# A Strassen-type MLP in a one-core decoder layer: paddings, weight sums in place, another order of products

## The chip, the cores and the metric

The kernel runs on one core of a Trainium2 chip. The metric is the device time of one execution in microseconds (us). A second figure is the span, from the first to the last instruction that the profiler recorded; one profiled execution gives both.

## The reference

One decoder layer in float32 with 1024 tokens and 1024 channels: x += gate1 * Mixer(h), x += gate2 * MLP(h), and a last RMSNorm. The part that the change is about:

```python
h = rmsnorm(x, norm2_g[l]) * (1.0 + scale2) + shift2
x = x + gate2 * (jnp.square(jax.nn.relu(h @ mlp_w1[l])) @ mlp_w2[l])     # 1024 -> 4096 -> 1024
return rmsnorm(x, final_g)
```

The mixer runs four branches (gated DeltaNet, pooling, spatial gating, retention) on one input projection, multiplies each branch's output by a sigmoid gate of the same input, adds them up and projects the sum.

## The kernel before

Everything lies channel by token: a tile is 128 channels of 512 tokens ("half" hf is 0 or 1). Each float32 operand is split into a rounded high part (ScalarE copy into float32r) and a low rest (VectorE subtraction), and a product is three matmuls: high by high, high by low, low by high (`mm3` at L125, L415 in the mixer, `product` at L1125).

Order of the stages: input projection, pooling and spatial gating; the mixers, whose short chains on VectorE and TensorE are filled up with matmuls of the projection (L415); `branches`, 64 units of a gate (24 matmuls, hh or hl by whi or wlo) and a branch product (12 matmuls, yh or yl by bh or bl); `outproj`; `mlp`.

The MLP uses Winograd's form of Strassen's scheme: in a 2 x 2 block product seven products take the place of eight. The operand sets b11, t3, n2, b21, n1, t4, b22 are sums of blocks of the activations (high and low parts, four tiles of 128 x 512 each), and a11, s3, s2, a12, s1, a22, s4 are sums of blocks of the weights. One product is 12 matmuls into a PSUM bank. `up` runs 16 units (p), each making a pair of 128-row blocks of the hidden layer for both halves; it squares the positive part, forms the sums that the second layer needs and stores them in DRAM (`ad`). `down` runs 4 x 4 units (c: quarter of the hidden layer, m: pair of output blocks); at each c the seven operand sets are loaded and split again (`load`, `put`). For p below NE (5) the products a11 x b11 and a12 x b21 run before the units, while VectorE still builds the other operand sets, and their results wait in `early` and in DRAM.

Weights come in `wpair` as two loads of 512 KB; s3 and s1 are added on VectorE, s2 and s4 on GpSimd (L1102), and each operand is split when its product is issued, into one of seven pairs of buffers (wh, wl). In `down`, `snap` scales a bank on ScalarE into v and adds v to x1 on GpSimd (L1137); x1 itself was saved to DRAM by `outproj` and is loaded again before `down`.

A scheduler orders each engine's instructions at build time, by program order among those that its model holds ready; on the chip each queue (SP's, which issues nearly all DMAs, among them) runs in that fixed order and waits on semaphores.

Pools are stacked from both ends of a partition. Their first bytes, as the program allocates them:

| pool | holds | first byte | beyond a multiple of 128 |
|---|---|---|---|
| cp (left) | small constants, rowb | 16,512 | 0 |
| bp | hh, hl, mh, ml, operand sets (tag h) | 21,120 | 0 |
| s4, later mp, later xb | plh, pll; mixer tiles; yh, yl, x1, operand sets (tag b16) | 86,656 | 0 |
| pb (right) | bh, bl, sig and others of `branches`, `outproj` | 159,616 | 0 |
| pm (right) | raw, wh, wl, st, early | 153,536 | 64 |
| wp (right) | raw, whi, wlo | 204,736 | 64 |

Of the kernel before, what the change touches and what calls it, by code (L numbers as in the profile page):

```python
# [63 lines left out]
def layout(x, c, positions, norm1_g, norm2_g, ada_w, ada_b, w_in, dn_conv_w, dn_a_log,  # L64
# [18 lines left out]
    o["w1"] = tiles(A["mlp_w1"][0])  # L83
    o["w2"] = ct(A["mlp_w2"][0].reshape(4, 4, 2, P, NB, P).transpose(0, 4, 3, 2, 1, 5).reshape(4, NB, P, 1024))
# [13 lines left out]
class Trunk:  # L98
# [90 lines left out]
    def start(self):  # L189
# [4 lines left out]
        self.rowb = cp.tile([P, 520], FP32, name="rowb")  # L194
# [822 lines left out]
    def outproj(self):  # L1017
# [7 lines left out]
        for hf in range(2):  # L1025
# [15 lines left out]
            ps = self.pss()  # L1041
            nc.tensor.matmul(out=ps, lhsT=self.one, rhs=ssq, start=True, stop=True)
            if hf == 0:
                rs = bp.tile([P, 512], FP32, tag="rs", name="rs", bufs=2)
                self.rms(ps, rs)
                self.S = {"b11": self.opset(self.xb, "b16"), "b21": self.opset(self.xb, "b16")}
        self.ps_rs = ps
# [4 lines left out]
    def put(self, op, k, x):  # L1052
        hi, lo = self.S[op][:, 0, k], self.S[op][:, 1, k]
        self.nc.scalar.copy(out=hi, in_=x)  # L1054
        self.nc.vector.tensor_tensor(out=lo, in0=x, in1=hi.bitcast(FP32), op=ALU.subtract)  # L1055
# [12 lines left out]
    def h2_rest(self, k, rs):  # L1068
        nc = self.nc
        self.h2_raw(1, k, rs, nc.vector)  # L1070
        self.h2_raw(1, k + 4, rs, nc.gpsimd)
        x11, x21, x12, x22 = self.x1[0][:, k], self.x1[0][:, k + 4], self.x1[1][:, k], self.x1[1][:, k + 4]
        tt = lambda eng, o, a, b: eng.tensor_tensor(out=o, in0=a, in1=b, op=ALU.subtract)
# [3 lines left out]
        tt(nc.vector, x11, x11, x12)  # L1077
        neg(n2, x22, x11)
        self.put("n2", k, n2)
        tt(nc.gpsimd, x12, x22, x12)  # L1080
        self.put("t3", k, x12)
        self.put("n1", k, x11)
        neg(x21, n2, x21)
        self.put("t4", k, x21)


    def st(self, name):
        return self.pm.tile([P, 512], FP32, tag="st", name=name, bufs=7)

    def wpair(self, s0, s1):  # L1090

        nc, pm = self.nc, self.pm
        r = []
        for s in (s0, s1):
            r.append(pm.tile([P, 1024], FP32, tag="raw", name="raw", bufs=2))
            nc.sync.dma_start(out=r[-1], in_=s)
        a11, a12, a21, a22 = r[0][:, :512], r[0][:, 512:], r[1][:, :512], r[1][:, 512:]
        src = {"a11": a11, "a12": a12, "a22": a22}

        def sums():  # L1100
            s = {n: pm.tile([P, 512], FP32, tag="sg", name=n, bufs=4) for n in ("s3", "s1", "s2", "s4")}
            add = lambda eng, o, a, b: eng.tensor_tensor(out=o, in0=a, in1=b, op=ALU.add)  # L1102
            add(nc.vector, s["s3"], a11, a21)
            add(nc.vector, s["s1"], a21, a22)
            add(nc.gpsimd, s["s2"], s["s1"], a11)
            add(nc.gpsimd, s["s4"], s["s2"], a12)
            src.update(s)

        def get(n):
            if n[0] == "s" and n not in src:  # L1110
                sums()
            hi = pm.tile([P, 512], FR, tag="wh", name="wh", bufs=7)
            lo = pm.tile([P, 512], FR, tag="wl", name="wl", bufs=7)
            self.split(src[n], hi, lo)
            return hi, lo
        return get
# [17 lines left out]
    def mlp(self):  # L1134
        nc, A, pm = self.nc, self.A, self.pm
        NP, NE = 16, 5
# [3 lines left out]
        OPS = ("b11", "t3", "n2", "b21", "n1", "t4", "b22")  # L1140
        ad = {(o, p): self.dp.tile([P, 512], FP32, name=f"ad_{o}_{p}") for o in OPS for p in range(NP)}
        store = lambda o, p, x: nc.sync.dma_start(out=ad[o, p], in_=x)
        rs = self.st("rs")
        self.rms(self.ps_rs, rs)
        for o in ("n2", "t3", "n1", "t4"):
            self.S[o] = self.opset(self.bp, "h")

        early = pm.tile([P, 8, 512], FP32, tag="ex", name="early", bufs=1)
        for p in range(NE):
            w = self.wpair_first(A["w1"][2 * p])  # L1150
            a, b = self.bank(), self.bank()
            self.product(a, w[0], "b11", True)
            nc.scalar.copy(out=early[:, p], in_=a)
            self.product(b, w[1], "b21", True)
            x = self.st("x11")
            tt(nc.vector, x, b, early[:, p], ALU.add)
            sq(x, x)
            store("b11", p, x)
            if p > 0:
                self.h2_rest(p - 1, rs)  # L1160
# [10 lines left out]
        def up(p, after):  # L1171
            e = p < NE
            get = self.wpair(A["w1"][2 * p], A["w1"][2 * p + 1])
            a, c = self.bank(), self.bank()

            def prod(ps, w, o, start):
                self.product(ps, get(w), o, start)
                after(o)
            if e:
                v1 = early[:, p]  # L1180
# [6 lines left out]
            prod(c, "s3", "t3", True)  # L1187
            x22 = self.st("x22")
            nc.scalar.copy(out=x22, in_=c)
            prod(a, "s2", "n2", e)  # L1190
            x21 = self.st("x21")
            if e:
                tt(nc.vector, x21, a, v1, ALU.add)
                tt(nc.gpsimd, x22, x22, v1, ALU.add)
                prod(c, "a22", "t4", False)
                stt(x21, c, -1.0, x21, ALU.mult, ALU.subtract)
            else:
                nc.scalar.copy(out=x21, in_=a)
                b = self.bank()
                prod(b, "a12", "b21", True)  # L1200
                tt(nc.vector, x11, b, x11, ALU.add)
                sq(x11, x11)
                store("b11", p, x11)
            prod(a, "s1", "n1", False)
            stt(x22, a, -1.0, x22, ALU.mult, ALU.subtract)
            if not e:
                prod(c, "a22", "t4", False)
                stt(x21, c, -1.0, x21, ALU.mult, ALU.subtract)
# [4 lines left out]
            prod(a, "s4", "b22", False)  # L1213
            x12 = self.st("x12")
            if e:
                tt(nc.vector, x12, a, v1, ALU.add)
                sq(x12, x12)
            else:
                nc.scalar.activation(out=x12, in_=a, func=AF.Relu)
                tt(nc.vector, x12, x12, x12, ALU.mult)  # L1220
# [10 lines left out]
        place = {"b11": (self.xb, "b16"), "b21": (self.xb, "b16"), "b22": (pm, "ex")}  # L1231

        def load(c, o):
            pool, tag = place.get(o, (self.bp, "h"))
            self.S[o] = self.opset(pool, tag, 1 if tag == "ex" else 4)
            for j in range(4):
                r = self.st("ar")
                nc.sync.dma_start(out=r, in_=ad[o, 4 * c + j])
                self.put(o, j, r)

        for p in range(NP):
            up(p, (lambda o: load(0, o)) if p == NP - 1 else (lambda o: None))
        x1 = [self.xb.tile([P, NB, 512], FP32, tag="b16", name="x1", bufs=4) for _ in range(2)]
        for d in range(NB):
            for hf in range(2):
                nc.sync.dma_start(out=x1[hf][:, d], in_=self.x1d[hf][d])
        ng = self.ng2 = self.cp.tile([P, 8], FP32, name="ng2")
        nc.vector.tensor_scalar_mul(out=ng, in0=self.modc[:, 40:48], scalar1=-1.0)
        ssq = [None, None]
        pq = [None, None]  # L1250

        def square(d, hf):
            x = x1[hf][:, d]
            if d == 0:
# [5 lines left out]
            if d < 6:  # L1260
                tt(nc.gpsimd, ssq[hf], ssq[hf], s, ALU.add)
                return
            if d == 6:
                pq[hf] = self.bank()
                nc.tensor.matmul(out=pq[hf], lhsT=self.one, rhs=ssq[hf], start=True, stop=False)
            nc.tensor.matmul(out=pq[hf], lhsT=self.one, rhs=s, start=False, stop=(d == 7))

        def down(c, m, after):
            get = self.wpair(A["w2"][c, 2 * m], A["w2"][c, 2 * m + 1])
# [4 lines left out]
            last = c == 3  # L1274

            def prod(ps, w, o, start):
                self.product(ps, get(w), o, start)
                after(o)

            def snap(ps, x, g):  # L1280
                v = self.st("v")
                nc.scalar.activation(out=v, in_=ps, func=AF.Copy, scale=g)  # L1282
                tt(nc.gpsimd, x, x, v, ALU.add)

            def add(ps, x, g):
                stt(x, ps, g, x, ALU.mult, ALU.add)
            prod(a, "a11", "b11", True)
            snap(a, x11, g0)
            prod(c_, "s3", "t3", True)
            snap(c_, x22, n1)  # L1290
            prod(a, "s2", "n2", False)
            snap(a, x21, n1)
            prod(b, "a12", "b21", True)
            add(b, x11, g0)
            prod(a, "s1", "n1", False)
            add(a, x22, n1)
            prod(c_, "a22", "t4", False)
            add(c_, x21, n1)
            prod(a, "s4", "b22", False)
            add(a, x12, g0)  # L1300
            if last:
                for d, hf in ((d0, 0), (d1, 0), (d0, 1), (d1, 1)):
                    square(d, hf)

        for c in range(4):
            for m in range(4):
                down(c, m, (lambda o: load(c + 1, o)) if m == 3 and c < 3 else (lambda o: None))
        for hf in range(2):
            rs = self.st("rs")
            self.rms(pq[hf], rs)  # L1310
            for db in range(NB):
                x = x1[hf][:, db]
                gf = self.prm[:, R_FG + db:R_FG + db + 1]
                if db in (1, 4, 7):
                    self.tc.keep_in_program_order(nc.scalar.activation(out=x, in_=x, func=AF.Copy, scale=gf))
                    nc.gpsimd.tensor_tensor(out=x, in0=x, in1=rs, op=ALU.mult)
                else:
                    stt(x, x, gf, rs, ALU.mult, ALU.mult)
# [3 lines left out]

    def wpair_first(self, s):

        r = self.pm.tile([P, 1024], FP32, tag="raw", name="raw", bufs=2)
        self.nc.sync.dma_start(out=r, in_=s)
        out = []
        for i in range(2):
            hi = self.pm.tile([P, 512], FR, tag="wh", name="wh", bufs=7)
            lo = self.pm.tile([P, 512], FR, tag="wl", name="wl", bufs=7)  # L1330
            self.split(r[:, i * 512:(i + 1) * 512], hi, lo)
            out.append((hi, lo))
        return out
# [70 lines left out]
```

## Time and profile before

| | us |
|---|---|
| three runs | 2065.03, 2067.99, 2066.51; median 2066.51 |
| the profiled execution | 2063.06 |
| its span | 2061.2 |
| mean granted TensorE clock | 0.977 of full speed |

The lines further down are from this one profiled execution. PE is TensorE's matmul, PEld its weight load, DVE is VectorE, ACT ScalarE, POOL GpSimd, SP the queue that issues DMAs. A group `out<-in` names tiles without their numbers. Matmuls overlap, so the distance of their starts says more than the duration of one. What follows `<-` is what ended an idle time.

### The profile page before, as it was taken

The page shows a single profiled execution, that of the slowest core. Times are in us where ns is not written, and L with a number is a line of the kernel's source. Part 1 is how long each engine was busy: PE and PEld are TensorE (multiplying, and loading weights), DVE is VectorE, ACT ScalarE, POOL GpSimd, SP SyncE. Part 2 cuts the span into 40 slices and gives each one's busy share as a digit, 9 for nine tenths or more (in the row PEclk, how much of TensorE's full clock was granted, in tenths as well). Part 3 has the DMA queues.
Part 4 walks back from the last instruction along what each step waited for, and adds up shares of the span by engine and source line. Part 5 has one row for each costly group of instructions (what it writes and reads, how often), then busy time and mean ns, then how long its engine had stood idle before and what let it go on. Part 6 is the DMA issues. An engine that isn't in the chain of part 4 may idle for free.

```text
span 2061.2 us, 24240 instructions
## 1 busy us (share of the span) xinstructions
PE 1948.1 (95%) x9004; PEld 1563.8 (76%) x9004; DVE 1223.0 (59%) x2132; ACT 688.1 (33%) x1177; POOL 407.5 (20%) x285
## 2 busy tenths in 40 slices
PE   5999989999999999999999999978999997999995
PEld 3888867777888888788788788756788876777774
DVE  7745679775744461252521324688866676758774
ACT  4523535332212221211211213542233343535442
POOL 4101211010000000021111112223211113435373
PEclk9999999998999999999999999988999998999998
DMA  7322121122222271251411213434444466424422
GB/s 274 129 83 92 45 54 47 49 64 71 62 72 62 72 235 46 79 182 52 148 68 41 92 41 113 153 110 156 166 146 158 144 223 211 164 92 153 163 83 81
DMA packets 125681, 230.56 MB, mean 112 GB/s; under 512 B 43126, under 2 KB 43766, under 8 KB 125564
## 3 DMA queue, kind: packets, MB, share of 16 engines
q1 hardware_dynamic: 124284, 224.83, 32.7%
q0 software_dynamic: 1280, 4.20, 0.9%
q8 instruction: 70, 1.15, 0.2%
q14 instruction: 47, 0.39, 0.1%
HBM read 177.06 MB, written 47.73 MB: 109 GB/s over the span
## 4 chain that ended last, share of the span: by engine, by line
PE 44%; DVE 6%; DMA 3%; ACT 2%; issue 1%; POOL 1%; DVEq 0%; SPq 0%; ACTq 0%; POOLq 0%
PE mm L125 22%; PE mm L1125 12%; PE sm L1125 11%; DVE op L1055 1%; DVE wl L110 1%; DVE x L1138 1%; DMA ar<-ad_n 1%; DMA raw<-in_w 1%; DVE s L1102 1%; DVE rs L187 0%; ACT op L1054 0%; POOL s L1102 0%; DMA ar<-ad_t 0%; ACT wh L109 0%; DVE x L1137 0%
## 5 line engine op out<-in xcount | busy, mean ns | idle before, releaser
L1125 PE MATMUL mm<-op,wh 128*128 128x512 f32 x928 | 297.2, 401 | 21.3 <-ACT wh L109 6.9
L1125 PE MATMUL sm<-op,wh 128*128 128x512 f32 x864 | 275.8, 399 | 20.9 <-ACT v L1282 12.0
L1125 PEld LDWEIGHTS mm<-op,wh 128*128 128x128 f32 x928 | 175.1, 191 | 71.9 <-ACT v L1282 10.8
L125 PE MATMUL mm<-hh,whi 128*128 128x512 f32 x560 | 221.8, 396 | 0.0
L125 PE MATMUL mm<-hh,wlo 128*128 128x512 f32 x560 | 221.5, 395 | 0.0
L125 PE MATMUL mm<-hl,whi 128*128 128x512 f32 x560 | 221.5, 395 | 0.0
L110 DVE TENSOR_TENSOR wlo<-raw,whi 128x1024 fp32r<-128x1024 f32 x86 | 106.9, 1244 | 183.1 <-ACT whi L109 173.7
L1125 PEld LDWEIGHTS sm<-op,wh 128*128 128x128 f32 x864 | 163.3, 190 | 63.3 <-ACT v L1282 13.5
L415 PE MATMUL mm<-hh,whi 128*128 128x512 f32 x512 | 209.3, 409 | 0.0
L415 PE MATMUL mm<-hh,wlo 128*128 128x512 f32 x512 | 209.3, 409 | 0.0
L415 PE MATMUL mm<-hl,whi 128*128 128x512 f32 x512 | 208.6, 407 | 0.0
L109 ACT CAST whi<-raw 128x1024 fp32r<-128x1024 f32 x88 | 92.1, 1048 | 336.5 <-PE mm L125 206.7
L1125 PE MATMUL mm<-op,wl 128*128 128x512 f32 x464 | 184.1, 398 | 1.3 <-DVE wl L110 1.3
L1125 PE MATMUL sm<-op,wl 128*128 128x512 f32 x432 | 171.9, 398 | 0.0
L997 POOL TENSOR_TENSOR acc<-acc,sig 128x512 f32<-128x512 f32 x48 | 66.6, 1388 | 530.8 <-DVE sig L996 523.3
L1102 POOL TENSOR_TENSOR s<-s,raw 128x512 f32<-128x512 f32 x64 | 98.2, 1534 | 317.2 <-DVE s L1102 223.9
L109 ACT CAST wh<-s 128x512 fp32r<-128x512 f32 x128 | 79.2, 620 | 210.5 <-PE sm L1125 66.7
L110 DVE TENSOR_TENSOR wl<-s,wh 128x512 fp32r<-128x512 f32 x128 | 110.8, 866 | 55.0 <-ACT wh L109 54.3
L125 PEld LDWEIGHTS mm<-hh,wlo 128*128 128x128 f32 x560 | 105.3, 188 | 25.4
L125 PEld LDWEIGHTS mm<-hh,whi 128*128 128x128 f32 x560 | 105.3, 188 | 25.2 <-issue 0.8
L125 PEld LDWEIGHTS mm<-hl,whi 128*128 128x128 f32 x560 | 105.3, 188 | 24.9
L996 DVE TENSOR_TENSOR sig<-sig,mm 128x512 f32<-128x512 f32 x48 | 33.0, 687 | 143.9 <-PE mm L125 143.9
(356 smaller groups left out, 3680.0 us busy)
## 6 DMA issues: line engine op xcount, KB each, us to landing
raw<-in_wt SPq DMA_DIRECT2D x80, 512.0 KB, 3.3
raw<-in_w SPq DMA_DIRECT2D x69, 512.0 KB, 3.8
adaw<-in_ada SPq DMA_DIRECT2D x64, 256.0 KB, 4.4
ad_b<-x SPq DMA_DIRECT2D x48, 256.0 KB, 2.5
ar<-ad_b SPq DMA_DIRECT2D x48, 256.0 KB, 4.1
adaw<-in_ada SPq DMA_DIRECT2D x16, 512.0 KB, 7.1
raw<-in_wbr SPq DMA_DIRECT2D x16, 512.0 KB, 3.9
yraw<-yd SPq DMA_DIRECT2D x32, 256.0 KB, 3.1
```

The costliest lines, as they stand in the source:

```text
L109: nc.scalar.copy(out=hi, in_=raw)
L110: (eng or nc.vector).tensor_tensor(out=lo, in0=raw, in1=hi.bitcast(FP32), op=ALU.subtract)
L125: self.nc.tensor.matmul(out=ps, lhsT=a, rhs=b, start=(i == 0), stop=(i == 3 * n - 1))
L415: self.nc.tensor.matmul(out=ps, lhsT=blk(a, k), rhs=r[hf][:, k], start=(k == 0 and i == 0), stop=(k == NB - 1 and i == 2))
L996: nc.vector.tensor_tensor(out=sg, in0=sg, in1=pb, op=ALU.mult)
L997: nc.gpsimd.tensor_tensor(out=a, in0=a, in1=sg, op=ALU.add)
L1055: self.nc.vector.tensor_tensor(out=lo, in0=x, in1=hi.bitcast(FP32), op=ALU.subtract)
L1102: add = lambda eng, o, a, b: eng.tensor_tensor(out=o, in0=a, in1=b, op=ALU.add)
L1125: self.nc.tensor.matmul(out=ps, lhsT=a, rhs=b, start=start and n == 0, stop=(n == 11), skip_group_check=True)
L1138: stt = lambda o, a, s, b, op0, op1: nc.vector.scalar_tensor_tensor(out=o, in0=a, scalar=s, in1=b, op0=op0, op1=op1)
```

## The change

The weights of both MLP layers are laid out in the order a22, a21, a11, a12, and one load brings all four (`wraw`). The sums are made in place on VectorE: (a22, a21) + (a21, a11) gives s1 and s3, then s2 and s4. Splits are made two operands wide (`halves`) into buffers that have one copy each for (a11, a12), (s1, s3), (s2, s4) and two for a22. `wprep` is a generator: each `step()` in a unit makes a part of the next unit's weights. NE is 8, and an early unit's second product adds into the bank of its first. The order of products and of the operand sets is another; at the end of `up` each set is loaded into the place freed one product before. GpSimd does nothing in the MLP any more. rowb moves to the pool cq (right, closed before the branches), the left padding is 128 bytes, and 64 bytes are put below pb on the right.

```diff
-        self.rowb = cp.tile([P, 520], FP32, name="rowb")
+        self.rowb = self.cq.tile([P, 520], FP32, name="rowb")
...
-        self.pad(ctx, "left", 32)
+        self.pad(ctx, "left", 128)
...
         self.xb = ctx.enter_context(tc.tile_pool(name="xb", bufs=1, reuse_waits="tile"))
+        self.pad(right, "right", 64)
         self.pb = right.enter_context(tc.tile_pool(name="pb", bufs=1, side="right", reuse_waits="tile"))
...
+    def halves(self, tag, raw, bufs):
+        n = raw.shape[1]
+        hi = self.pm.tile([P, n, 512], FR, tag=tag + "h", name=tag + "h", bufs=bufs)
+        lo = self.pm.tile([P, n, 512], FR, tag=tag + "l", name=tag + "l", bufs=bufs)
+        self.split(raw, hi, lo)
+        return [(hi[:, i], lo[:, i]) for i in range(n)]
...
+    def wprep(self, src, W, early=False):
+        add = lambda o, a, b: nc.vector.tensor_tensor(out=o, in0=a, in1=b, op=ALU.add)
+        raw = self.wraw(src)
+        yield
+        if not early:
+            W["a11"], W["a12"] = self.halves("a", raw[:, 2:4], 1)
+        W["a22"], = self.halves("d", raw[:, 0:1], 2)
+        yield
+        add(raw[:, 0:2], raw[:, 0:2], raw[:, 1:3])
+        add(raw[:, 2], raw[:, 0], raw[:, 2])
+        add(raw[:, 3], raw[:, 2], raw[:, 3])
+        yield
+        W["s1"], W["s3"] = self.halves("g", raw[:, 0:2], 1)
+        yield
+        W["s2"], W["s4"] = self.halves("c", raw[:, 2:4], 1)
+        yield
...
-        NP, NE = 16, 5
+        NP, NE = 16, 8
...
+        def asq(o, x):
+            nc.scalar.activation(out=o, in_=x, func=AF.Relu)
+            nc.scalar.activation(out=o, in_=o, func=AF.Square)
...
         for p in range(NE):
+            if p + 2 < NE:
+                w.append(self.halves("agc"[(p + 2) % 3], self.wraw(A["w1"][p + 2], slice(2, 4))[:, 2:4], 1))
+            first(p)
+            if p == 0:
+                ps = self.bank()
+                nc.tensor.matmul(out=ps, lhsT=self.one, rhs=self.ssq2, start=True, stop=True)
+                rs = self.st("rs")
+                self.rms(ps, rs)
+            else:
+                second(p - 1)
+                if p < 5:
+                    self.h2_n2(p - 1, rs)
...
+            step()
...
+            step()
             prod(a, "s2", "n2", e)
...
+            prod(c, "s3", "t3", True)
...
+            step()
             prod(a, "s1", "n1", False)
...
+            step()
+            prod(c, "a22", "t4", False)
...
+            prod(a, "s4", "b22", False)
+            step()
...
             def snap(ps, x, g):
+                if c == 0:
+                    nc.scalar.activation(out=x, in_=ps, func=AF.Copy, scale=g)
+                    return
                 v = self.st("v")
                 nc.scalar.activation(out=v, in_=ps, func=AF.Copy, scale=g)
-                tt(nc.gpsimd, x, x, v, ALU.add)
+                tt(nc.vector, x, x, v, ALU.add)
...
+            if c == 1:
                 for d, hf in ((d0, 0), (d1, 0), (d0, 1), (d1, 1)):
+                    r = self.st("x1r")
+                    nc.sync.dma_start(out=r, in_=self.x1d[hf][d])
+                    tt(nc.vector, x1[hf][:, d], x1[hf][:, d], r, ALU.add)
```

`down` runs a11, a12, s2, s3, s1, a22, s4, and the last unit a11, s3, s2, a12, a22, s1, s4, with the squares of each output block as soon as it is complete. `h2_n2` and `h2_t3` are `h2_rest` in two parts, all on VectorE; the last RMSNorm's products are on VectorE alone.

## Rows read from the trace of the kernel before

**Rows 1.** The page: busy time, share and instructions of each engine.

```profile
PE 1948.1 (95%) x9004; PEld 1563.8 (76%) x9004; DVE 1223.0 (59%) x2132; ACT 688.1 (33%) x1177; POOL 407.5 (20%) x285
```

**Rows 2.** Timeline of TensorE (start, us, operation), first and 42nd matmul.

```profile
72.23 0.40 PE L125 MATMUL mm<-hh,wlo 128*128 128x512 f32 x1
...
81.80 0.39 PE L125 MATMUL mm<-hl,whi 128*128 128x512 f32 x1
```

**Rows 3.** The same, 84 to 95 us: first and 50th matmul.

```profile
83.66 0.39 PE L125 MATMUL mm<-hh,plh 128*128 128x512 f32 x1
...
94.78 0.39 PE L125 MATMUL mm<-hl,plh 128*128 128x512 f32 x1
```

**Rows 4.** Chain that ended last, in order of time (start, us, what).

```profile
874.01 126.18 PE mm L125 x543
...
2020.05 8.40 PE mm L1125 x36
...
2031.25 2.74 PE mm L1125 x12
```

**Rows 5.** Groups by line: busy us, mean ns, idle us before.

```profile
L125 PE MATMUL mm<-hh,whi 128*128 128x512 f32 x560 | 221.8, 396 | 0.0
...
L415 PE MATMUL mm<-hh,whi 128*128 128x512 f32 x512 | 209.3, 409 | 0.0
...
L125 PE MATMUL mm<-mh,whi 128*128 128x512 f32 x128 | 50.6, 395 | 0.0
```

**Rows 6.** Busy time by stretch: PE, PEld, DVE, ACT, POOL (x instructions), clock, DMA, GB/s.

```profile
1345.00:1400.00 55.00, 37.79 (x137) 28.39 (x138) 50.67 (x68) 28.87 (x51) 16.41 (x10) 0.81 0.32 110
1400.00:1480.00 80.00, 75.03 (x311) 58.57 (x310) 69.74 (x94) 19.90 (x34) 23.14 (x15) 0.98 0.51 173
1480.00:1660.00 180.00, 180.00 (x773) 144.25 (x772) 118.49 (x185) 58.45 (x103) 29.69 (x20) 1.00 0.45 150
1660.00:1740.00 80.00, 66.56 (x270) 51.85 (x269) 58.24 (x84) 36.15 (x62) 18.83 (x13) 0.91 0.69 230
...
1855.00:1880.00 25.00, 21.96 (x87) 16.94 (x87) 24.62 (x32) 17.54 (x32) 8.40 (x6) 0.93 0.68 229
```

**Rows 7.** TensorE's waits: total us, times, longest us.

```profile
PE sm L1125 <- ACT v L1282: 12.0, 2, 11.5
...
PE sm L601 <- DVE kt L579: 7.7, 2, 5.9
```

**Rows 8.** Timeline, 1343 to 1350 us, from the output projection to the MLP.

```profile
1343.52 0.39 PE L125 MATMUL mm<-mh,wlo 128*128 128x512 f32 x1
...
1345.14 20.58 SPq L1326 DMA_DIRECT2D raw<-in_w  x5
...
1349.72 1.22 PE L1125 MATMUL mm<-op,wh 128*128 128x512 f32 x2 [2.26 <-ACT wh L109]
```

**Rows 9.** Groups of the MLP by line; the last row has min/median/max ns.

```profile
L110 DVE TENSOR_TENSOR wl<-s,wh 128x512 fp32r<-128x512 f32 x128 | 110.8, 866 | 55.0 <-ACT wh L109 54.3
L1102 POOL TENSOR_TENSOR s<-s,raw 128x512 f32<-128x512 f32 x64 | 98.2, 1534 | 317.2 <-DVE s L1102 223.9 <-ACT op L1054 37.6 <-ACT x L1186 17.9
...
L110 DVE TENSOR_TENSOR wl<-s,wh x128: 672/685/1827, 1392.4 to 2015.2; 128x512 fp32r<-128x512 f32 x128
```

**Rows 10.** Timeline of ScalarE and VectorE, single operations and a run of three.

```profile
1332.52 1.05 ACT L109 CAST whi<-raw 128x1024 fp32r<-128x1024 f32 x1 [3.31 <-PE mm L125]
1333.60 1.23 DVE L110 TENSOR_TENSOR wlo<-raw,whi 128x1024 fp32r<-128x1024 f32 x1
...
1687.87 1.88 DVE L1055 TENSOR_TENSOR op<-ar,op 128x512 fp32r<-128x512 f32 x3
```

**Rows 11.** Timeline behind the last product.

```profile
2037.38 4.20 DVE L187 RECIPROCAL rs<-rs 128x128 f32<-128x128 f32 x5 [2.60 <-ACT rs L185]
...
2042.79 13.97 SPq L1320 DMA_DIRECT2D out_dram<-x  x8
```

More of the change, by code (lines that the diff above doesn't have):

```diff
@@ L1084, in h2_rest @@
-        self.put("t4", k, x21)
     def st(self, name):
[L1088 to L1116, printed above, removed]
@@ L1144, in mlp @@
-        self.rms(self.ps_rs, rs)
         for o in ("n2", "t3", "n1", "t4"):
             self.S[o] = self.opset(self.bp, "h")
+        w = []
+        for p in range(2):
+            w.append(self.halves("agc"[p % 3], self.wraw(A["w1"][p], slice(2, 4))[:, 2:4], 1))
         early = pm.tile([P, 8, 512], FP32, tag="ex", name="early", bufs=1)
-        for p in range(NE):
[L1150 to L1160, printed above, removed]
+        banks = []
@@ new lines, in first, with second @@
+        def first(p):
+            banks.append(self.bank())
+            self.product(banks[p], w[p][0], "b11", True)
+            nc.scalar.copy(out=early[:, p], in_=banks[p])
+        def second(p):
+            self.product(banks[p], w[p][1], "b21", False)
+            x = self.st("x11")
+            asq(x, banks[p])
+            store("b11", p, x)
+        for p in range(NE):
+            if p + 2 < NE:
[10 more added lines that the diff above has]
+                    self.h2_n2(p - 1, rs)
+                elif p == 5:
+                    for k in range(4):
+                        self.h2_t3(k)
+                elif p == 6:
+                    for k in range(4):
+                        self.put("n1", k, self.x1[0][:, k])
@@ L1169, in fresh, with up @@
             return sums[:, ns[0] % 8]
-        def up(p, after):
+        def up(p, W, nxt, after):
             e = p < NE
-            get = self.wpair(A["w1"][2 * p], A["w1"][2 * p + 1])
             a, c = self.bank(), self.bank()
+            step = lambda: nxt and next(nxt)
             def prod(ps, w, o, start):
-                self.product(ps, get(w), o, start)
+                self.product(ps, W[w], o, start)
                 after(o)
+            step()
             if e:
-                v1 = early[:, p]
                 x11 = self.st("x11")
@@ L1186, in up @@
                 nc.scalar.copy(out=x11, in_=a)
-            prod(c, "s3", "t3", True)
-            x22 = self.st("x22")
-            nc.scalar.copy(out=x22, in_=c)
+                b = self.bank()
+                prod(b, "a12", "b21", True)
+                tt(nc.vector, x11, b, x11, ALU.add)
+                asq(x11, x11)
+                store("b11", p, x11)
+            step()
             prod(a, "s2", "n2", e)
@@ L1273, in down @@
             a, c_, b = self.bank(), self.bank(), self.bank()
-            last = c == 3
+            step = lambda: nxt and next(nxt)
             def prod(ps, w, o, start):
-                self.product(ps, get(w), o, start)
+                self.product(ps, W[w], o, start)
                 after(o)
             def snap(ps, x, g):
+                if c == 0:
+                    nc.scalar.activation(out=x, in_=ps, func=AF.Copy, scale=g)
+                    return
                 v = self.st("v")
@@ L1291, in down @@
+            step()
             prod(a, "s2", "n2", False)
             snap(a, x21, n1)
-            prod(b, "a12", "b21", True)
-            add(b, x11, g0)
+            if end:
+                prod(b, "a12", "b21", True)
+                add(b, x11, g0)
+                square(d0, 0)
+                prod(c_, "a22", "t4", False)
+                add(c_, x21, n1)
+                square(d1, 0)
+            else:
+                prod(c_, "s3", "t3", True)
+                snap(c_, x22, n1)
+            step()
@@ L1295, in down @@
             prod(a, "s1", "n1", False)
             add(a, x22, n1)
-            prod(c_, "a22", "t4", False)
-            add(c_, x21, n1)
-            prod(a, "s4", "b22", False)
-            add(a, x12, g0)
-            if last:
-                for d, hf in ((d0, 0), (d1, 0), (d0, 1), (d1, 1)):
+            if end:
+                square(d1, 1)
+            step()
+            if not end:
+                prod(c_, "a22", "t4", False)
+                add(c_, x21, n1)
+            prod(a, "s4", "b22", False)
@@ new lines, in down @@
+            if c == 0:
+                nc.scalar.activation(out=x12, in_=a, func=AF.Copy, scale=g0)
+            else:
+                add(a, x12, g0)
+            step()
+            if c == 1:
+                for d, hf in ((d0, 0), (d1, 0), (d0, 1), (d1, 1)):
+                    r = self.st("x1r")
+                    nc.sync.dma_start(out=r, in_=self.x1d[hf][d])
+                    tt(nc.vector, x1[hf][:, d], x1[hf][:, d], r, ALU.add)
+            if c == 3:
+                for d, hf in ((d0, 1),) if end else ((d0, 0), (d1, 0), (d0, 1), (d1, 1)):
@@ L1306, in mlp @@
             for m in range(4):
-                down(c, m, (lambda o: load(c + 1, o)) if m == 3 and c < 3 else (lambda o: None))
+                turn = m == 3 and c < 3
+                N = {}
+                nxt = None if (c, m) == (3, 3) else self.wprep(A["w2"][4 * c + m + 1], N)
+                after = lambda o: None
+                if turn:
+                    after = lambda o: load(c + 1, o)
+                down(c, m, W, nxt, after)
+                W = N
         for hf in range(2):
```

152 lines of the change are left out of this document (82 added, 70 removed).

## The prediction

> **What bounds the kernel now.** I read the engines' totals first, then the chain of waits, then TensorE's starts in the timeline, then stage tables. The reader is to see TensorE busy for 95% of the span, nothing else above 59% [rows 1]: the time is the number of matmuls times the distance from one start to the next, plus the stretches in which TensorE waits. Both can be read.
>
> *The distance.* At full clock two values occur. Between 72.23 and 81.80 us 41 matmuls hh x whi follow one another: 9.57 / 41 = 233.4 ns [rows 2]. A moment later the same hh with the weights plh makes 49 starts in 11.12 us: 226.9 ns [rows 3]. The MLP has the slow value: 36 in 8.40 us, 233.3 ns [rows 4]. Shape, type and clock are the same; what differs is where the operands lie. Adding up the tiles as the program allocates them, bp (hh, hl, most operand sets), xb and s4 (plh, pll) begin at a multiple of 128 bytes (bp at 21,120 = 165 x 128), wp (whi, wlo) and pm (MLP weights) at 64 beyond one. hh x plh has both operands in one class, hh x whi and op x wh have them in two. Two more pairs fit: yh x bh (xb and pb, both multiples of 128) inside the branches, and b22 x s4 in the down phase, where the operand set lies in pm beside its weights (both 64 beyond): 12 in 2.74 us against 2.80 [rows 4].
>
> *The waits.* MLP products start at 1349.72 [rows 8] and the last one ends at 2031.25 + 2.74 = 2034.0 [rows 4], 684.3 us. The work is 2496 x 0.2334 + 192 x 0.2283 = 626.4 us, so 57.9 us are lost. The stage table places them [rows 6], each as length less matmuls x 0.2334: 1349.7 to 1400 about 19 (55 less the 4.7 ahead of the first product, and some 133 products' matmuls), 1400 to 1480 7.4, 1480 to 1660 nothing, 1660 to 1740 17.0, each of three turns of the down phase about 3.6 (one is shown: 25 - 87 x 0.2334 = 4.7; the others by the same table 3.4 and 2.8), some 3 elsewhere. In the first two VectorE is busy 50.7 of 55 and 69.7 of 80 us; in the third one wait of 11.5 us [rows 7] lies behind the reload of operand sets.
>
> **The change, part by part.**
>
> 1. *Paddings.* rowb (2080 bytes) leaves cp, the left padding grows from 32 to 128: bp, s4, mp and xb move by -1984 bytes = -15.5 x 128, to 64 beyond 128. The new 64 bytes on the right move pb likewise. wp and pm stay. All large pairs are then in one class, so 226.9 ns. Gates and branches: 543 matmuls took 126.18 us [rows 4], 232.4 each; 5.5 x 2304 = 12.6 us. Output projection 3 x 128 [rows 5] x 6.5 = 2.5. The remaining 192 with wp weights: 3 x 560 [rows 5] and 48 into `sm` less the gates' 1536, x 6.5 = 1.2. L415, 3 x 512 [rows 5] x 6.5 = 10.0, of which I take 7: TensorE waits 7.7 us for VectorE's kt there [rows 7], and whatever lies before such a wait only lengthens it. MLP 2496 x 6.5 = 16.2. Sum 39.5. From both sides: 0 if it isn't the addresses, 43 if everything counts; I take the nearest rows, hh with two partners. VectorE shows no such classes (L1055 into sets at multiples of 128 takes 0.69 [rows 10], L110's wl in pm at 64 beyond 685 ns in the median [rows 9]), so nothing is booked for it. One more memset on GpSimd and the moved rowb load are off every chain.
>
> Against this stands the Trainium skill: "SBUF — State Buffer" (Door 1, the note on cachelines) has engine reads go by 16-byte lines, and "TensorE: Matmul & The Clock Gate" (Step-by-step: what each phase is for) gives weights and moving operand a read port each, so that loading the one takes nothing from the other. By these, a shift by 64 bytes changes nothing, part 1 is 0, and the 6.5 ns in rows 2 and 3 would need another cause. The trace has the difference, with the same hh; the rule is kept as a rival.
>
> 2. *GpSimd out of the MLP.* Its adds took 1.53 us each, and VectorE's 512-wide splits beside them 866 ns on average [rows 9], where the median is 685; back to back three take 1.88 us, 0.60 from start to start [rows 10]; a 1024-wide one is 1.23, I take 1.13 from start to start. VectorE now also does the sums s2 and s4, the snaps' adds, x21 - x12 and the squares' sums. Per late unit of `up`: 3 wide splits, 1 wide sum, 12 narrow = 11.7 of TensorE's 7 x 2.72 = 19.1 us. Per early unit (now 8, 5 products): 3 wide and 14 narrow = 11.8 of 13.6 us, tight. Per unit of `down` 8.3 (c = 0), 13.1 (c = 1, with four x1 adds), 10.7 after. ScalarE gets Relu and Square; at 58 of 180 us in the steady stretch [rows 6] it is no bound.
>
> 3. *More early products, another order.* Before the units, 16 products (43.6 us) instead of 10 stand ready, accumulated in the bank without an add. VectorE has about 44 us there: reciprocals 3.4, splits 9.0, n2 group 14.4, t3, n1, t4, b22 12.0, first weight set 5.2. All but t4 and b22 is due by the end of the products, so the 15 us hole near 1390 is covered; if VectorE lags, its lag is late there. I keep 12 of the 26.6 us lost up to 1480: 2.5 for a slow clock and the first wl, 3 at the change to the units, 6.5 in the early units. Gain 14.6.
>
> 4. *Weights one unit ahead.* One 1 MB load instead of two of 512 KB; hi/lo are written while the unit before runs. Pairs a, g and c have one buffer. c is rewritten after s4, 1.05 + 1.23 us plus two releases [rows 10], 2.5 in all; in late units and `down` two products (5.4 us) lie between, in early ones only s3, if it is run ahead of s2 (in the 6.5 above). Behind a waiting split on ScalarE stand the copies that empty the banks, and TensorE waits for those.
>
> 5. *Up to down.* Operand sets for c = 0 need only units 0 to 3; b11 goes to the room of `early` ahead of unit 15, every other set into the place freed one product earlier. The 16 x1 reloads leave this place for c = 1, and c = 0 writes x1 by ScalarE alone. Of 17.0 us I keep 4, for x1 waiting on the last stores of `sums`. Gain 13.
>
> 6. *Turns.* 28 loads and puts (16.8 us VectorE) meet two units: 8.3 + 16.8 + 13.1 = 38.2 us of TensorE's 38.1, then 40.6, then 38 or more. DMA is at 0.68 of its time in such a stretch [rows 6]. I expect 12 us where 10.9 are lost now: -1.1.
>
> 7. *Ends.* At the start, the ones matmul and the reciprocals leave the path, but the first weights are still loaded behind the last x1d store on SP (issue 1345.14 [rows 8]) and split 1024 wide: +0.5, and the ones matmul comes back between products, +1.1. At the end hf 0 is complete two products earlier. From the last product: add 0.75, square, ones matmul, Sqrt (3.4 in all); VectorE then still owes hf 0's 8 products; reciprocals (0.84 each [rows 11]) and 8 more end at about 15, the last store 4.4 later, as now (2042.79 + 13.97 to 2061.2): 19.5 instead of 27.2. Eight ones matmuls move between products: +3.4. Net -2.7 for both ends.
>
> *Sum.* Elsewhere 1 of the 3 us is regained. -39.5 - 14.6 - 13 + 1.1 - 2.7 - 1 = -69.7. The profiled span 2061.2 becomes 1991.5. That execution took 2063.06, 1.9 more than its span; the runs shown have a median of 2066.51, 5.3 above the span; so 1996.8, 1997 us.
>
> **The rivals.**
>
> - *The addresses aren't it.* For: the rule above; for the class "both 64 beyond" only b22's 192 matmuls speak. Against: rows 2 and 3. 39.5 less: 2036. Chance 0.09.
> - *VectorE becomes the bound.* If its instructions don't overlap, an early unit holds 14 x 0.69 + 3 x 1.23 = 13.4 of 13.6 us; with 0.2 us of release at half of them 15.1, 8 x 1.5 = 12, and the turns cost some 8 more: 2017. For: 13 and 14 narrow instructions in strict order, and evacuations queued behind splits. Against: the 0.60 spacing. 0.20.
> - *All is covered.* Stalls fall from 30 to 12: 1979. For: 1480 to 1660 runs without a gap now. Against: the turns' traffic. 0.16.
> - *Slower:* a, g and c have one buffer where seven pairs stood. If the rewrite of c (2.5 us) ends up in TensorE's path in all 32 units, 80 us are lost: 2077. From 70 / 32 = 2.2 us per unit it decides the sign. For: ScalarE must run a 1024-wide copy just then, behind whatever is queued. Against: two products of cover in 24 of 32 units. 0.05.
>
> My forecast has 0.50, its own range 1985 to 2010. 8 times in 10: 1972 to 2024, which takes in the covered case, the VectorE case, and leaves out the two worst and the far ends of the others. About 0.2% is what can be told from no change. Faster by more: 0.94, all but the slower rival and 0.01 of far ends; of those 0.06, 0.04 are slower and 0.02 within it.
>
> **What would show it.** Starts of hh x whi, op x wh and L415 227 ns apart, branches 126.2 -> 123.2 us per 543: part 1; 233 refutes it. No hole near 1390 (some 25 us earlier) and VectorE's narrow instructions at 685 ns on average: parts 2, 3. Waits of `sm`/`mm` on ScalarE's ch or VectorE's cl at each unit's first product: the slower rival. A wait above 5 us at the first `down` unit: part 5 wrong. Holes of 3 to 5 us at c = 1, 2, 3: part 6. Last product to end below 22 us: part 7. A time above 2030 means that part 1 or the cover failed.

## The result and the profile after

The changed kernel takes 2011.35 us (median of 4, 2008.77 to 2016.73) against 2065.77 for the kernel before: ratio 0.974, interval 0.972 to 0.976. Forecast were 1997 and a range of 1972 to 2024. The profiled execution spans 2008.1 us, 53.1 less than before, where the working had 69.7.

The engines' totals of the changed kernel; GpSimd fell from [rows 1] to 177 us, VectorE hardly changed:

```profile
span 2008.1 us, 23759 instructions
PE 1912.8 (95%) x9004; PEld 1558.7 (78%) x9004; DVE 1218.6 (61%) x2114; ACT 703.5 (35%) x1121; POOL 176.9 (9%) x145
```

Its chain in order of time (start, us, what), answering [rows 4]: the MLP went from 8.40 to 8.16 us per 36 matmuls, the branches from 126.18 only to 125.06 per 543:

```profile
865.74 125.06 PE mm L128 x543
...
1517.42 8.16 PE mm L1136 x36
```

Its stretches (columns as in [rows 6]). Length less matmuls x 0.2274 us (the mean distance of starts in this MLP) gives what is lost: 4.7 us up to 1385 (behind the first product at 1336.6), 3.6 up to 1500, nothing up to 1640, 10.4 where up becomes down, 6.1 at the second turn, from c = 1 to c = 2:

```profile
1334.00:1385.00 51.00, 47.47 (x192) 38.15 (x193) 47.17 (x65) 38.88 (x62) 0.00 (x0) 0.90 0.44 150
1385.00:1500.00 115.00, 113.39 (x490) 90.63 (x489) 94.40 (x131) 33.84 (x42) 0.00 (x0) 1.00 0.58 196
1500.00:1640.00 140.00, 140.00 (x619) 115.92 (x618) 95.74 (x123) 58.95 (x83) 0.00 (x0) 1.00 0.49 159
1640.00:1700.00 60.00, 53.30 (x218) 40.77 (x217) 40.70 (x56) 31.81 (x50) 0.00 (x0) 0.97 0.65 218
...
1820.00:1845.00 25.00, 20.37 (x83) 16.24 (x83) 21.45 (x30) 9.58 (x16) 0.00 (x0) 0.93 0.43 150
```

TensorE's waits in it from 1300 us on (us, times, longest), answering [rows 7]. No split of the c pair (cl) is among the long ones:

```profile
PE mm L1136 <- DVE al L113: 5.5, 2, 4.6
PE sm L1136 <- ACT v L1342: 3.3, 4, 1.5
PE mm L1136 <- ACT ah L112: 3.2, 1, 3.2
PE sm L1136 <- ACT op L1060: 3.0, 1, 3.0
```

Piece by piece, from the starts of first and last products:

| piece | working | measured |
|---|---|---|
| up to the last output-projection matmul | -23.3 | 1343.52 to 1329.49: -14.0 |
| from there to the first MLP product | +0.5 | 6.20 to 7.10: +0.9 |
| MLP products | -39.2 | 684.3 to 647.75: -36.5 |
| from the last product to the end | -7.7 | 27.2 to 23.75: -3.5 |

Of the 16.6 us missed, 9.3 lie ahead of the MLP and 4.2 in the tail. Inside the MLP two errors nearly cancel: the early stretches lost less than booked, the way from up to down more.

### The profile page after: what moved, and what is told of

Same layout as the page of the kernel before. It is cut to its first block, busy times and chain, and to the rows that moved or that the text cites. A ratio compares the mean times of both kernels' runs of the same rounds, so it can differ in the third digit from the quotient of the medians.

```text
span 2008.1 us, 23759 instructions
## 1 busy us (share of the span) xinstructions
PE 1912.8 (95%) x9004; PEld 1558.7 (78%) x9004; DVE 1218.6 (61%) x2114; ACT 703.5 (35%) x1121; POOL 176.9 (9%) x145
## 4 chain that ended last, share of the span: by engine, by line
PE 46%; DVE 5%; DMA 4%; issue 2%; ACT 1%; SPq 0%; DVEq 0%; ACTq 0%
PE mm L128 22%; PE mm L1136 12%; PE sm L1136 11%; DMA ar<-ad_b 2%; DVE op L1061 1%; DVE x L1149 1%; DMA ar<-ad_t 1%; DVE x L1148 1%; DVE rs L190 1%; DMA x<-ad_b 0%; DVE raw L1113 0%; ACT op L1060 0%; DMA ar<-ad_n 0%; DMA yraw<-yd 0%; DVE dl L113 0%
## 5 line engine op out<-in xcount | busy, mean ns | idle before, releaser
L128 PE MATMUL mm<-hl,whi 128*128 128x512 f32 x560 | 218.5, 390 | 0.0
L418 PE MATMUL mm<-hh,wlo 128*128 128x512 f32 x512 | 206.3, 403 | 0.0
L418 PE MATMUL mm<-hh,whi 128*128 128x512 f32 x512 | 206.2, 403 | 0.0
L418 PE MATMUL mm<-hl,whi 128*128 128x512 f32 x512 | 205.6, 402 | 0.0
L128 PEld LDWEIGHTS mm<-hh,wlo 128*128 128x128 f32 x560 | 105.5, 188 | 23.3
L128 PEld LDWEIGHTS mm<-hh,whi 128*128 128x128 f32 x560 | 105.5, 188 | 22.8 <-issue 0.8
L128 PEld LDWEIGHTS mm<-hl,whi 128*128 128x128 f32 x560 | 105.5, 188 | 22.8
L418 PEld LDWEIGHTS mm<-hh,wlo 128*128 128x128 f32 x512 | 97.7, 191 | 17.5
L418 PEld LDWEIGHTS mm<-hl,whi 128*128 128x128 f32 x512 | 97.5, 190 | 17.6
L418 PEld LDWEIGHTS mm<-hh,whi 128*128 128x128 f32 x512 | 97.5, 191 | 17.5 <-issue 0.5
L973 ACT ACTIVATE sig<-mm 128x512 f32<-128x512 f32 x64 | 38.0, 594 | 205.7 <-PE mm L128 150.9
L1136 PE MATMUL sm<-op,ch 128*128 128x512 f32 x336 | 104.9, 393 | 2.8 <-ACT v L1342 2.5
L128 PE MATMUL mm<-yh,bh 128*128 128x512 f32 x256 | 101.7, 397 | 3.3 <-ACT yh L112 3.3
L128 PE MATMUL mm<-yl,bh 128*128 128x512 f32 x256 | 101.3, 396 | 0.1
L128 PE MATMUL mm<-yh,bl 128*128 128x512 f32 x256 | 100.9, 394 | 0.0
L1136 PE MATMUL mm<-op,gh 128*128 128x512 f32 x288 | 91.4, 396 | 2.3 <-ACT x L1239 1.4
```

What stands on the lines that cost most here:

```text
L128: self.nc.tensor.matmul(out=ps, lhsT=a, rhs=b, start=(i == 0), stop=(i == 3 * n - 1))
L418: self.nc.tensor.matmul(out=ps, lhsT=blk(a, k), rhs=r[hf][:, k], start=(k == 0 and i == 0), stop=(k == NB - 1 and i == 2))
L973: nc.scalar.activation(out=sg, in_=pg, func=AF.Sigmoid)
L1136: self.nc.tensor.matmul(out=ps, lhsT=a, rhs=b, start=start and n == 0, stop=(n == 11), skip_group_check=True)
```

## The experiments

Theory A: a 128x128 by 512 matmul follows the last one after 227 ns only if its moving operand and its weights start a multiple of 256 bytes apart. Theory B: 128 bytes, as predicted. Theory C: addresses don't count. The tile addresses give, for starts modulo 256 (moving, weights), these mean distances over starts under 300 ns apart: 233.3 at (128, 192) before; 226.8 to 228.3 at (192, 192) after; and yh x bh 229.0 at (128, 128) before, but 232.9 at (192, 64) after.

**e1: the distance by itself.**

```
for s in range(4):
    for m in range(16):
        series(weights + 64 * s bytes, moving + 32 * m bytes, n=24)
```

> This kernel leaves the whole computation out: it runs 64 series of 24 products of 128x128 weights with a 512-column operand (same type as in the kernel) one behind the other; the weights start 0, 64, 128 or 192 bytes beyond a place, the moving operand 0, 32, ... 480 bytes beyond another place of the same class modulo 256. Theory A (what counts is the difference of the two starts modulo 256 bytes): in each of the four groups of 16 series the starts are 227 ns apart at the two offsets where the difference is a multiple of 256 and 233 ns apart at differences of 64, 128 and 192; the differences of 32, 96, ... are open. Theory B (the class modulo 128, as predicted): 227 ns at four of 16 offsets, also where the difference is 128. Theory C (the addresses don't count): one value for all 64 series.

The timeline of the series with the weights at 0 (start, us, what); a series' start to the next one's, over 24, is the distance. The last letter counts 32 bytes each:

```profile
29.62 5.60 PE L124 MATMUL sama<-mv,st 128*128 128x512 f32 x24
35.06 5.77 PE L124 MATMUL samb<-mv,st 128*128 128x512 f32 x24
40.66 5.67 PE L124 MATMUL samc<-mv,st 128*128 128x512 f32 x24
46.16 5.77 PE L124 MATMUL samd<-mv,st 128*128 128x512 f32 x24
51.78 5.76 PE L124 MATMUL same<-mv,st 128*128 128x512 f32 x24
57.38 5.78 PE L124 MATMUL samf<-mv,st 128*128 128x512 f32 x24
...
74.19 5.63 PE L124 MATMUL sami<-mv,st 128*128 128x512 f32 x24
79.66 5.77 PE L124 MATMUL samj<-mv,st 128*128 128x512 f32 x24
```

At difference 0 the next series follows 5.44 us later (226.7 ns each), at 256 5.47 (227.9; behind its eighth matmul 226.7 too), at 128 5.60 (233.3). Unexpected: 64 beyond the weights is nearly fast (5.50, 229.2), 64 short of them is not (233). The other three groups repeat it, shifted with the weights. A holds but for the difference of +64, where it said 233; B and C fall. The Trainium skill's rule weighed in the prediction ("SBUF — State Buffer", Door 1, with "TensorE: Matmul & The Clock Gate", Step-by-step) would give one value; the trace disagrees by 6.6 ns.

**e2 and e3: the paddings alone, and the change without them.** e2 is the kernel before with the three lines of the paddings. e3 is the changed kernel with

```
-self.pad(ctx, "left", 128)
+self.pad(ctx, "left", 64)
-self.pad(right, "right", 64)
```

> The kernel before with the paddings of the change alone (rowb in the other pool, 128 bytes on the left, 64 more on the right). Theory A (difference modulo 256): all large pairs fast but yh x bh, which goes from 229 to 233 ns; filler -8, gates, branches and output projection -6, MLP 2304 x 6.3 ns = -14.5: about 2037 us. Theory B (modulo 128): -39.5, 2026 us. Theory C: 2066 us.

> The changed kernel with every pool back in the class of the kernel before (64 bytes on the left, none more on the right; rowb stays where the change put it, for its room). Theory A: +8 filler, +6 branches and output projection, +14.5 MLP, about 2040 us. Theory B: +39.5, 2051 us. Theory C: 2011 us.

e2 2047.21 us (ratio 0.991, interval 0.988 to 0.993), e3 2033.42 (0.985, 0.982 to 0.989). C is out; both lie nearer A's number than B's, though e2 is 10 slower and e3 7 faster than A said. e2's product phase (first start to last start) fell only from 683.9 to 679.9 though its starts came closer by 1536 x 5.9 + 960 x 6.6 ns = 15.4 us: the down phase, 303 us each, holds the same 1217 matmuls in the kernel before (first) and in e2 (second):

```profile
1740.00:2043.00 303.00, 289.94 (x1217) 227.54 (x1215) 209.81 (x271) 142.48 (x244) 134.48 (x81) 0.99 0.35 118
```

```profile
1720.00:2023.00 303.00, 287.84 (x1217) 230.06 (x1215) 214.53 (x271) 142.75 (x244) 129.70 (x81) 0.98 0.36 118
```

What TensorE gained there it waited; which engine paces it was not tested. In the new MLP the same paddings are worth 661.4 - 647.4 = 14.0 us. In the whole time the two parts, 33 us for the new MLP without the paddings (e3) and 19 for the paddings alone, make 52 of 54. That they add up is chance as far as single executions tell: in the product phase they make 22.5 + 4.0 of 36.5, ahead of it 5.5 + 16.3 of 14.0.

**e4: the branches' pair brought together.** `self.pad(right, "right", 64)` becomes 192.

> The changed kernel with 192 bytes of padding on the right in place of 64, so that the branches' operand sets and weights both start 192 beyond a multiple of 256. Theory A: 768 matmuls yh x bh at 227.5 in place of 232.9 ns, -4.2, about 2007 us. Theory B (same class modulo 128 already): 2011 us, no change. Theory C: no change.

2000.51 us (0.969, 0.966 to 0.971), 11 less than the changed kernel. The same place of the chain, 543 matmuls of gates and branches, now takes:

```profile
860.71 123.40 PE mm L128 x543
```

The working had 123.2. yh x bh came to 226.8 ns, as A said; the gates, whose own addresses didn't move, also fell, from 227.9 to 226.8, which A as put doesn't explain. The starts do: behind slow matmuls a fast pair needs some seven starts to reach its own distance. One unit of yh x bh in the kernel before, first, seventh, and the gate behind the twelfth:

```profile
1107.17 0.39 PE L125 MATMUL mm<-yh,bh 128*128 128x512 f32 x1
...
1108.56 0.39 PE L125 MATMUL mm<-yh,bh 128*128 128x512 f32 x1
...
1109.92 0.40 PE L125 MATMUL mm<-hh,whi 128*128 128x512 f32 x1
```

That is 231.7 ns each for six, then 226.7. Over all units it is 231.5 and 226.7; the changed kernel's gates, behind slow yh x bh, have 231.0 in their first seven and 226.7 after; in e4, where no pair is slow, both have 226.7 to 226.9 from the first on. So 229.0 was a mean of two parts, and yh x bh slowed the gates as well. The two falls make 768 x 6.1 + 1536 x 1.1 = 6.4 us. The branches stage is 8.7 us shorter; the other 2 are within what single executions of the mixers differ.

**e5: the tail** (on e4, as e6 to e8): half 0's norm inside the last unit.

```
 square(d1, 0)
+rs = self.st("rs"); self.rms(pq[0], rs)
 ...
 square(d1, 1)
+finish(0, rs, range(4))      # 4 of half 0's products and their stores
```

> On the kernel with 192 bytes on the right (2000.5 us): the norm of half 0 is issued inside the last unit as soon as its sum of squares is complete, four of its eight products before the last sum of half 1, four after it. Theory A (the end is long because half 0's root stands behind half 1's last square in ScalarE's order): half 0's reciprocals and products run beside the last two products, from the last square 0.7 to the sum, 1.8 to the root, 3.4 reciprocals, 5.4 products, 4.4 store: the end falls by about 7, 1993.5 us. Rival B (the last half's own chain and the stores set it, whatever half 0 does): not under 1999 us. Rival C (half 0's work on VectorE delays half 1's last sums by as much): 1998 us.

The changed kernel's end: half 0's root waits in ScalarE's order behind half 1's last square, though its sum was in the bank some 7 us before:

```profile
1985.23 0.63 ACT L1317 ACTIVATE sq<-x 128x512 f32<-128x512 f32 x1 [4.13 <-DVE x L1149]
1985.76 0.67 ACT L188 ACTIVATE rs<-sm,eps 128x512 f32<-128x512 f32 x1
...
1986.46 4.20 DVE L190 RECIPROCAL rs<-rs 128x128 f32<-128x128 f32 x5 [1.33 <-ACT rs L188]
...
1990.58 5.29 DVE L1149 SCALAR_TENSOR_TENSOR x<-x,prm,rs 128x512 f32<-128x512 f32 x8
...
1998.39 5.39 DVE L1149 SCALAR_TENSOR_TENSOR x<-x,prm,rs 128x512 f32<-128x512 f32 x8
```

e5's: the first root 11 us ahead of the second, and one run of 8 products behind the last:

```profile
1966.92 0.69 ACT L188 ACTIVATE rs<-sm,eps 128x512 f32<-128x512 f32 x1 [1.22 <-PE sm L1324]
...
1978.24 0.69 ACT L188 ACTIVATE rs<-mm,eps 128x512 f32<-128x512 f32 x1 [1.22 <-PE mm L1324]
1978.96 3.39 DVE L190 RECIPROCAL rs<-rs 128x128 f32<-128x128 f32 x4 [1.28 <-ACT rs L188]
1982.39 5.39 DVE L1149 SCALAR_TENSOR_TENSOR x<-x,prm,rs 128x512 f32<-128x512 f32 x8
```

1994.78 us, -5.7 by the medians; by the ratios (0.967, 0.965 to 0.970) some 3, and the intervals overlap. The traces show it in its place: from the last product to the end 16.5 us where 23.75 stood, while the product phase grew from 646.7 to 650.7. A, with a part of C: half 0's reciprocals stand ahead of a sum of half 1, and TensorE waits 2.8 us for it.

**e6: the first operand set of down loaded earlier.** `if last:` around `load(0, "b11")` becomes `if p == 12:`.

> On the kernel with 192 bytes on the right (2000.5 us): the first operand set of the down phase is loaded before unit 12 instead of unit 15. Theory A (the stretch 1640 to 1700 loses 10.8 instead of 4 us because a product of the down phase stands in unit 15 ahead of its operand set, and the clock then falls): the wait of 3 us on ScalarE's puts at about 1640 and the slow stretch behind it go, -3 to -6, about 1996 us. Rival B (the reloads of the other six sets and the stores ahead of them set this stretch): 1999 to 2001 us.

2003.45 us: no gain. The wait on the b11 puts is gone, and a longer one stands there, on a copy that empties a bank:

```profile
PE mm L1136 <- ACT x L1239: 6.2, 1, 6.2
```

Ahead of the copy on ScalarE stands a put of the next set whose data hadn't landed:

```profile
1635.00 0.62 ACT L1060 CAST op<-ar 128x512 fp32r<-128x512 f32 x1 [2.81 <-DMA ar<-ad_b]
```

A falls as put: the wait it named went, but the next set's data were late too.

**e7: the x1 additions off the turn.** `if c == 1:` becomes `if c in (1, 2) and m in (1, 2):`, each time for another pair.

> On the kernel with 192 bytes on the right (2000.5 us): the 16 additions of the stored x1 stand in the two middle units of c = 1 and c = 2 instead of all four units of c = 1, so that none stands in a unit beside a turn. Theory A (at the turn from c = 0 to c = 1 VectorE's queue sets the wait of 4.1 us on al and the slow clock behind it): -4 to -6, about 1995.5 us, and that wait is under 1 us. Rival B (the turn is bound by the 28 loads and puts themselves): the wait stays and the time is 1999 to 2001 us.

2004.15 us: not faster. The turn meant is the second, from c = 1 to c = 2, and not the one that the expectation names: the wait on al stands ahead of the MLP's 2057th matmul, and c = 2 starts with the 2017th. That wait did go from 4.1 to 1.1 us, and 1800 to 1850 holds 212 matmuls where e4 has 195; but the product phase fell only 1.8 us, since later stretches lost more, and the branches, whose code is the same, took 5 us longer in this execution. A right in its place, not in the time.

**e8: s2 and s4 on GpSimd again.**

```
-add(raw[:, 2], raw[:, 0], raw[:, 2])
-add(raw[:, 3], raw[:, 2], raw[:, 3])
+nc.gpsimd.tensor_tensor(out=raw[:, 2], in0=raw[:, 0], in1=raw[:, 2], op=ALU.add)
+nc.gpsimd.tensor_tensor(out=raw[:, 3], in0=raw[:, 2], in1=raw[:, 3], op=ALU.add)
```

> On the kernel with 192 bytes on the right (2000.5 us): the weight sums s2 and s4 run on GpSimd again. Theory A (GpSimd's adds slow VectorE's beside them and lengthen the chain of the weights): VectorE's narrow splits are at about 800 ns on average instead of 685, the early units and the turns lose, +5 to +10, about 2007 us. Rival B (taking GpSimd out was worth nothing to the time, since VectorE has room in the late units): 1999 to 2002 us. Rival C (VectorE is the bound, and is relieved of 2 x 0.6 us per unit): 1990 us.

2021.56 us (2010.56 to 2027.33), +21: more than A said, though the narrow splits came only to 732 ns and not 800; B and C fall. The product phase took 15.9 us more. VectorE's instructions in e8's MLP (busy, mean ns):

```profile
L1061 DVE TENSOR_TENSOR op<-ar,op 128x512 fp32r<-128x512 f32 x112 | 77.0, 732 | 16.0 <-ACT op L1060 15.6
L113 DVE TENSOR_TENSOR cl<-raw,ch 128x1024 fp32r<-128x1024 f32 x34 | 46.7, 1374 | 9.5 <-ACT ch L112 9.3
...
L1148 DVE TENSOR_TENSOR sums<-x,x 128x512 f32<-128x512 f32 x16 | 18.8, 1172 | 1.3 <-ACT x L1154 1.2
```

Without GpSimd (e4) these are 687, 1222 and 689. GpSimd's own adds take 1312 and 1694 ns. The Trainium skill ("SBUF — State Buffer", SBUF: two separate sides) says that a two-input VectorE instruction and a GpSimd one lock each other out of a shared port for a whole instruction; sums at 1172 on average, 691 to 1776, agree. How much is that and how much the longer chain s2, s4, c split was not separated.

**e9 and e11: why the operand sets are late** (both on e5). In e9 their loads are issued by GpSimd, in e11 they land in the low half's place:

```
-r = self.st("ar")
+r = self.S2[o][:, 1, j].bitcast(FP32)     # e11
-nc.sync.dma_start(out=r, in_=ad[o, 4 * c + j])
+nc.gpsimd.dma_start(out=r, in_=ad[o, 4 * c + j])     # e9
```

> On the kernel with the early norm (1994.8 us): the 112 loads of operand sets for the down phase are issued by GpSimd, which has nothing else to do there, in place of SP, where they stand in a fixed order behind stores that wait for units of the up phase. Theory A (what ended the wait when the b11 set was loaded early was a copy on ScalarE behind a put whose data came late, because its load was issued late on SP): the stretch from up to down loses 4 to 6 us less, the turns 1 to 3 less, about 1989 us. Rival B (the data are late for another reason, the free place in the rotating buffers or the transfers themselves): 1993 to 1997 us. Rival C (loads issued by GpSimd are slower or disturb VectorE as its adds did): over 2000 us.

> On the kernel with the early norm (1994.8 us, loads on SP): each load of an operand set for the down phase lands in the low half's own place and is split there, so it needs no place in the buffer of six that rotates among all temporaries of the units. Theory A (with the loads on GpSimd's queue 108 us of its waits were for VectorE to free that buffer: the rotation is what makes the data late, and copies on ScalarE wait behind the puts): the stretch from up to down loses 4 us less and the turns 2 to 4 less, about 1988 us. Rival B (the loads wait for the operand place itself, one product before, and SP for stores): 1993 to 1997 us.

e9 took 2010.25 us (ratio 0.972, 0.969 to 0.974), e11 1989.37 (0.962, 0.960 to 0.965); e5 has 0.967 (0.965 to 0.970), so by the ratios, which take out what the chips differ, e9 is some 9 us slower than e5 and e11 some 10 faster. The product phase is 9.9 longer and 8.3 shorter. In e9 GpSimd's queue, with nothing else in it, shows what its loads wait for (us, times): VectorE freeing the rotating temporaries. One of the 43 waits, 42.2 us, lies between the loads for c = 0 and those of the first turn, so what e11's expectation took as 108 us of lateness is at most 66.

```profile
  POOL ar L1285: 108.1, 43
```

Without that buffer the way from up to down holds 288 matmuls in 70 us (e11, second), 259 with it (e5, first):

```profile
1630.00:1700.00 70.00, 63.23 (x259) 48.58 (x260) 47.31 (x63) 36.16 (x55) 0.00 (x0) 0.98 0.58 190
```

```profile
1630.00:1700.00 70.00, 67.24 (x288) 54.50 (x287) 47.99 (x64) 34.94 (x54) 0.00 (x0) 0.98 0.50 184
```

The rotation is the cause, not SP's order: in e11 the loads stay on SP, behind stores of the up phase. Why e9 is slower than e5 was not taken apart.

**e10 and e12: combined.** e10 is e9 with e7's edit and the last square but one added on VectorE instead of by a ones matmul; e12 is e11 with these and e6's edit.

> The kernel with the early norm and the loads on GpSimd's queue, and with them the x1 additions off the turn and one ones matmul less per half (its summand is added on VectorE). Theory A (each wait goes by itself): x1 additions -2 as the product phase showed (646.65 to 644.81), 2 ones matmuls of 1.1 us each -2.2, about 4 us under the kernel with the loads on GpSimd's queue. Rival B (turns stay bound by loads and puts, and VectorE's extra adds lengthen the end): no difference to it within 2 us.

> The kernel with direct loads, and with the b11 set loaded before unit 12, the x1 additions off the turn and one ones matmul less per half. Theory A: the waits at the change to the down phase and at the turn from c = 0 to c = 1 go, and 2.2 us of ones matmuls: 4 to 7 us under the kernel with direct loads alone. Rival B (where one wait goes, the next copy behind a put takes its place, as when the b11 set alone was early): within 2 us of it.

2014.75 (0.975) and 1990.23 us (0.963, 0.960 to 0.965): neither is faster than its base. In e12 the stretch 1800 to 1850 is nearly full (218 matmuls), but 1900 to 1970 loses what was won, with waits of up to 3.6 us on VectorE's last sums. e11 stays the fastest, 1989.4 us against 2011.4 and 2065.8.

## Why the prediction was right, and where it was off

*Direction and mechanism* held: the distance falls with the paddings, and the waits shrink with the new MLP. "The addresses aren't it" is refuted by e1 and e3. "VectorE becomes the bound" didn't come about: the early units lost 3.6 us, and VectorE is busy 95.7 of 140 us after them. "Slower" neither: cl is among no long wait. "All is covered" came true in the early units alone.

*Part 1 is the mis-sized term*, at the step "all large pairs are then in one class, so 226.9 ns". The class is modulo 256, not 128. Rows 2 to 4 held only differences of 0 and 64, so both readings fitted, and the padding put yh x bh 128 apart. Counts times distances give -31.6 where 39.5 stood: gates, output projection and `sm` 2112 x 5.4 = 11.4, L418 1536 x 5.2 = 8.0, MLP 1536 x 5.8 + 960 x 6.4 = 15.0, b22 0.2, less yh x bh 768 x 3.9 = 3.0. Ahead of the MLP that is 16.4, which e2's execution shows (16.3) and the changed kernel's nearly does (14.0); e4 regained the branches. How much of L418's 8.0 came through stays open: L418 ended 8.25 us earlier than before, but 6.5 earlier in e3 too, without the paddings, and executions of the changed kernel and of e4 to e12, with the same mixer code, end it anywhere from 697.1 to 704.2 us.

*Part 2* carried more than its text priced: with two adds per unit back on GpSimd (e8) the early stretch holds 449 matmuls in 115 us where e4 has 487.

*Part 3*: 12 us kept, about 8 lost (4.7 and 3.6 in the two first stretches). Better than booked by 3.7; with part 5 worse by 6.4 and part 6 better by 1.4 it is luck that the MLP's forecast is only 2.7 off.

*Part 4*: right; no long wait is for the rewrite of a single buffer (that on al is part 6's).

*Part 5*: 4 us kept, 10.4 lost. "For x1 waiting on the last stores of `sums`" named the wrong wait; a product of the down phase stood in unit 15 ahead of its puts, and these waited for loads held up by the rotation of six temporaries (e6, e9, e11):

```profile
1637.33 4.67 SPq L1285 DMA_DIRECT2D ar<-ad_b  x6
...
1643.49 1.28 ACT L1060 CAST op<-ar 128x512 fp32r<-128x512 f32 x2 [5.53 <-DMA ar<-ad_b]
...
1644.16 0.50 PE L1136 MATMUL sm<-op,ah 128*128 128x512 f32 x1 [2.99 <-ACT op L1060]
```

Behind this wait the stretch's granted clock is 0.97, not 1.00 as in the 140 us before it.

*Part 6*: 12 expected, 10.6 lost at the three turns (1.6, 6.1, 2.9). The working had the second as the tightest, 40.6 us of VectorE in 38.1; there, five puts and an x1 addition stand ahead of the split of al:

```profile
1825.61 3.09 DVE L1061 TENSOR_TENSOR op<-ar,op 128x512 fp32r<-128x512 f32 x5
...
1828.62 0.69 DVE L1148 TENSOR_TENSOR x<-x,x1r 128x512 f32<-128x512 f32 x1
1829.22 1.22 DVE L113 TENSOR_TENSOR al<-raw,ah 128x1024 fp32r<-128x1024 f32 x1
...
1830.50 0.79 PE L1136 MATMUL mm<-op,al 128*128 128x512 f32 x1 [4.63 <-DVE al L113]
```

*Part 7*: the tail was taken as 19.5 us, with half 0's norm starting when its sum is complete. The program writes it after the last unit, so in fixed order it started when half 1 was nearly complete: 23.75. e5 showed it.

## What to carry to other kernels

Place moving operands and weights a multiple of 256 bytes apart, work out the class of every large pair after a padding (a shift that helps three pairs can hurt a fourth), and test a period at its half before booking it. A gain per instruction is worth what the stage lets through: the same paddings gave 4 us in an MLP that waited much and 14 in one that waited less. Where a wait goes, look in the engine's fixed order for what stands next, and ask of every late load which buffer it waits for before moving its issue.

## What the hardware showed

The distance of 512-column matmuls depends on the two start addresses with a period of 256 bytes, and not symmetrically. Behind the eighth matmul of a series it is 226.7 ns at differences of 0 and 256, 228.9 at +64 (moving operand beyond the weights), and 233.1 to 234.3 at every other multiple of 32, -64 and 128 among them (e1).

The place itself doesn't count where the difference is 0: 226.7 ns in all four groups of e1, whose places are 64 bytes apart. That yh x bh had 229.0 at (128, 128) comes from the matmuls ahead: behind a slow pair the first six or seven starts of a fast one are 231.0 to 231.5 ns apart on average, the later ones 226.7. So a slow pair costs some time in its neighbour too (e4). Why it takes so many starts was not tested.
